# An attention layer in banded steps: query factors and the high parts of streamed weights formed on GpSimd, three key copies on ScalarE, in place of VectorE

## The chip, the cores and the metric

The program runs on one core of one Trainium2 chip. A core has five engines that each work through a queue of their own in order: TensorE (PE in the profile, its weight loads PEld), VectorE (DVE), ScalarE (ACT), GpSimd (POOL) and SyncE (SP), which only issues transfers. The metric is the time of one execution in microseconds; the median of the runs is compared.

## What is computed

A trunk of two layers on 1024 tokens of width 1024 in float32. Layer 0 mixes tokens by a gated short convolution, layer 1 by attention in a sliding window of 128 with 16 query heads, 4 key heads and head width 64; a SwiGLU channel mixer follows each. Cut to the attention, which the change touches:

```python
qkv = h @ w_qkv
q = rmsnorm(q, q_gain)                   # over each head's 64 numbers
k = rmsnorm(k, k_gain)
scores = jnp.einsum('bnqkgd,bnskd->bnkgqs', qb, kw).astype(jnp.float32) * scale
alibi = -slopes[:, :, None, None] * dist.astype(jnp.float32)[None, None]
scores = scores + alibi[None, None]
scores = jnp.where(mask[None, :, None, None], scores, -jnp.inf)
logits = jnp.concatenate([scores, sink_col], axis=-1)
p = jax.nn.softmax(logits, axis=-1)[..., :-1]
out = jnp.einsum('bnkgqs,bnskd->bnqkgd', p.astype(vw.dtype), vw)
return out.reshape(bsz, s, N_Q_HEADS * HEAD_DIM) @ w_o
```

## The kernel before

Every float32 product is made of three matmuls of a faster format (fp32r): each operand is split into a high part (a cast, hi) and a low part (the number less its high part, lo), and hi x hi, hi x lo and lo x hi are summed. Large products are further cut by a scheme of seven products of quarter matrices, so that some weights are streamed as sums of quarters.

The attention layer is `attention_layer`. Keys and values are projected first, under a planner that gives each piece a due time. Then the instructions are issued by hand, in an order written out (`manual_schedule`), and each engine's queue is just what was issued to it. This part makes the queries of eight pairs of heads, and at the same time works the heads already made, in steps of one unit (head i, block b of 128 queries). One call of `step` goes through the letters of `ORDER = "ASPTMEDkPHLVOPK"`: for step n, A forms the distances of unit n+2 (GpSimd, L2261 and L2264: distance times a factor `away` of the head), S the scores of unit n (PE, L2249 and L2250, into the only bank P0), P one piece of the pair product (PE, L2036: 12 matmuls for each granule of streamed weights, taken from a doubled buffer WL), T turns the exponentials of unit n-2 (PE, L2305), M takes the scores and distances together and finds their maxima (VectorE, L2276), E the exponentials of unit n-1 (ScalarE, L2296), D the divisions that are due, k and K what is planned for this step, H and L the high and low part of the turned unit n-2 (ScalarE L2312, VectorE L2318), V the values' product of unit n-3 (PE, L2331 and L2332), and O its copy out (ScalarE L2349, VectorE L2350).

The divisions begin with the sink of two heads' half: `mx` less the sink (GpSimd, L2360), its exponential (ScalarE, L2361), added to the sums `den` (GpSimd, L2362). Later the inverse sums are spread (GpSimd, L1822), turned (PE, L1827) and multiplied in (VectorE, L2378).

Planned work is of four kinds. `split_granule` splits the next granule of streamed weights, hi on VectorE (L1979) and lo on GpSimd (L1980). `keep_q` makes a head's query tile: squares on ScalarE, their sums on PE (L1678), the mean `hr_m` on VectorE (L1719), its logarithm (ScalarE, L1697) and with an exponential (L1702) a first guess `hr_y` of the inverse root; VectorE squares it (L1704), improves it by a Newton step (L1724, L1725) and forms `away` (L1728). `keep_q` also splits the raw queries, in quarters, hi on ScalarE (L2202) and lo on GpSimd (L2207). `part` makes the key operands of two groups of heads g in halves e: a copy on ScalarE (L1912), a copied high part on VectorE (L1914), the low part on GpSimd (L1917), and a copy of it on ScalarE. `split_o` splits the finished output (ScalarE L2460, GpSimd L2461).

Of the kernel before, what the change touches and what calls it, by code (L numbers as in the profile page):

```python
# [15 lines left out]
P = 128  # L16
# [71 lines left out]
def trunk_kernel(ctx: ExitStack, tc: tile.TileContext, xT, small, w_in, w_out, w_q, w_v, w_o, w_gu, w_dn, out):  # L88
# [1571 lines left out]
    def attention_layer():  # L1660
# [39 lines left out]
        def head_guess(y):  # L1700

            act.activation(y, y, AF.Exp, scale=-0.5)  # L1702
            t = slot("hr_t", (P, NB, 2), bufs=2)
            dve.tensor_tensor(t, y, y, ALU.mult)  # L1704
            return t
# [13 lines left out]
                    dve.scalar_tensor_tensor(m[to, :, sub], src[of, :, e], 1.0 / HD, it["eps_q"][to, :, sub], ALU.mult, ALU.add)  # L1719
            return m  # L1720

        def query_newton(i, y, t, m):

            dve.scalar_tensor_tensor(t, t, 0.5, m, ALU.mult, ALU.mult)  # L1724
            dve.scalar_tensor_tensor(y, t, 1.5, y, ALU.subtract, ALU.mult)  # L1725
            minus[i] = y
            away[i] = slot("away", (P, NB, 2), bufs=3)
            dve.scalar_tensor_tensor(away[i], m, cst[:, C_NEGS + i : C_NEGS + i + 1], y, ALU.mult, ALU.mult)  # L1728

        minus = {}  # L1730
        away = {}
# [126 lines left out]
        def keys_and_values():  # L1858


            def load(name, src, n, t):
                def f():
                    it[name] = Weights()
                    nc.sync.dma_start(it[name].raw.rearrange("p (k c) -> p k c", k=n), src)

                at(t, f)

            def split_v(q):
                raw = it["wv", q].raw
                hi, lo = (slot(f"G{8 + 2 * i + q}", dtype=F32R) for i in (0, 1))  # L1870
                dve.tensor_copy(hi, raw)
                dve.tensor_tensor(lo, raw, plain(hi), ALU.subtract)
                it.setdefault("wv", []).append((hi, lo))

            t = begin
            at(t - 150.0, act.preload_act_table_set, "natural_log_exp_and_others")
            at(t - 20.0, constants)
            at(t + 9.0, lambda: nc.sync.dma_start(x_aside, X[NK - 1]))
            for q in (0, 1):
                load(("wv", q), w_v[:, 4 * q : 4 * q + 4, :], 4, t + (-14.0, -12.5)[q])  # L1880
                at(t + (-9.3, -6.6)[q], split_v, q)
            operand_sums(0, ("A2", "A3"), t - 4.6)
            operand_sums(1, ("A0", "A1"), t + 1.5)
            operand_sums(2, ("A4", "A5"), t + 8.0)

            def mean():
                ps = bank("P3")
                for b in range(NB):
                    c = slice(b % 4 * P, (b % 4 + 1) * P)
                    pe.matmul(ps[:, b : b + 1], state["ss", b // 4][:, c], ones, start=True, stop=True)  # L1890
                it["ps"] = ps

            def token_rows():
                m = slot("rs_m", (P, NB))
                it["r"], it["eps"] = slot("r", (P, NB)), slot("eps_r", (P, NB))
                dve.tensor_scalar(m, it["ps"][:, 0:NB], 1.0 / D, EPS, ALU.mult, ALU.add)
                dve.tensor_scalar(it["eps"], m, EPS, None, ALU.mult)
                it["eps_q"] = slot("eps_q", (P, NB, 2))
                for e in range(2):
                    for sub in range(2):  # L1900
                        of = it["eps"][sub * SUB : (sub + 1) * SUB, :]
                        dve.tensor_copy(it["eps_q"][e * SUB : (e + 1) * SUB, :, sub], of)
                rsqrt(it["r"], m, (P, NB))

            def part(g, e, i):
                if g not in kz:
                    kz[g] = pair_slot(f"A{g}"), pair_slot(f"A{g + 2}")
                hi, lo = kz[g]
                raw = key_raw[g]
                rows, rest = (slice(x * HD, (x + 1) * HD) for x in (e, 1 - e))  # L1910
                if i == 0:
                    act.copy(hi[rows, e, :], raw[rows, :])  # L1912
                elif i == 1:
                    dve.tensor_copy(hi[rest, e, :], raw[rows, :])  # L1914
                elif i == 2:
                    eng = dve if (g, e) == (0, 0) else pool
                    eng.tensor_tensor(lo[rows, e, :], raw[rows, :], plain(hi[rows, e, :]), ALU.subtract)  # L1917
                else:
                    act.copy(lo[rest, e, :], plain(lo[rows, e, :]))

            it["part"] = part

            def project_values(q):
                def f():
                    it["v", q] = project_v(q)

                line.work(51, f)

            project_values(0)
            line.work(4, mean)  # L1930
            at(line.end + 0.05, token_rows)
            project_values(1)
            operand_sums(3, ("G8", "G10", "G9", "G11"), line.end + 0.1)
            first_pairs()
# [104 lines left out]
        def first_pairs():  # L2039
# [61 lines left out]
            for j in range(n_first):  # L2101
                begins[j] = line.end
                u, k = seq[j]
                for p in range(NK // 2):
                    line.work(3, of_product, j, p)
                    if p == 1 and j == 7:
                        rows_work(0, 0)
                    if p == 1 and j == 8:
                        stats_work(1)
                    if p == 1 and j == 10:  # L2110
                        rows_work(1, 1)
                    if (j, p) in ((11, 3), (12, 0), (12, 1), (12, 2)):
                        line.work(1, first.stats, {(11, 3): 4, (12, 0): 6, (12, 1): 0, (12, 2): 2}[j, p], 2)
                    if (j, p) == (12, 2):
                        for d, f in ((0.1, first.mean), (0.5, first.guess), (0.9, first.newton)):
                            at(line.end + d, f)
                t = line.end
                finish(u, k, lambda f, t=t: at(t + 0.05, f))
                if j in (4, 6):
                    g = 0 if j == 4 else 1  # L2120
                    for h in (0, 1):
                        at(t + 0.8 + 0.65 * h, squares, g, h)
                if j == 5:
                    stats_work(0)
                if j in (7, 9):
                    rows_work(*{7: (0, 1), 9: (1, 0)}[j])
                if j == 9:
                    for i, d in enumerate((0.7, 0.06, 1.6, 3.1)):
                        at(t + d, it["part"], 0, 0, i)
                if j == 10:  # L2130
                    at(t + 0.4, keep_v, 0, 0)
                    at(t + 0.8, first.squares1)
                if j == 11:
                    at(t + 0.75, first.squares0)
                    at(t + 0.8, keep_v, 0, 1)
# [27 lines left out]
        def keep_q(i, raw_of, side=None, later=0, hold=0, steps=False):  # L2163
# [3 lines left out]
            def squares(h):  # L2167
                if "raw" not in t:
                    t["raw"] = raw_of()
                    wide = slot(f"G{5 + i % 2}") if side is None else side  # L2170
                    t["side"] = [wide[:, h * 512 : h * 512 + 512] for h in (0, 1)]
                act.activation(t["side"][h], t["raw"][:, h * 512 : h * 512 + 512], AF.Square)
# [8 lines left out]
                t["m"] = query_mean(t["st"])  # L2181
                t["y"] = head_log(t["m"])

            def guess():
                t["t"] = head_guess(t["y"])

            def newton():
                query_newton(i, t["y"], t["t"], t["m"])


            def halves(e):
# [17 lines left out]
            if steps:  # L2209
                return SimpleNamespace(  # L2210
                    squares1=lambda: squares(1),
                    squares0=lambda: squares(0),
                    stats=stats_of,
                    mean=mean,
                    guess=guess,
                    newton=newton,
                    hi0=lambda: part_hi(0, 0),
                    hi1=lambda: part_hi(0, 1),
                    hi2=lambda: part_hi(1, 0),
                    hi3=lambda: part_hi(1, 1),  # L2220
                    lo0=lambda: part_lo(0, 0),
                    lo1=lambda: part_lo(0, 1, dve),
                    lo2=lambda: part_lo(1, 0),
                    lo3=lambda: part_lo(1, 1),
                )
            for d, f in ((1, lambda: squares(0)), (1.5, lambda: squares(1)), (2.5, stats_of), (2.5, mean), (3, guess), (3, newton)):
                plan(d + later, f)
            for n, (h, e) in enumerate(((0, 0), (0, 1), (1, 0), (1, 1))):
                d = later + hold + 2 + n + 0.5 * (n > 0)
# [173 lines left out]
        def plan(d, f):  # L2403

            agenda.setdefault(pos["step"] + d, []).append(f)
# [91 lines left out]
        def work_of_pairs():  # L2497
            n = 0
            for j in range(n_first, len(seq)):
                u, k = seq[j]  # L2500
                plan(0, lambda j=j: split_granule(j + 1, dve, pool) if j > n_first else None)
                if j > n_first:
                    load_granule(j + 2)
                for p in range(NK // 2):
# [200 lines left out]
```

## Time and profile before

| | |
|---|---|
| median of 3 runs | 1939.04 us (1938.13 to 1940.21) |
| the profiled execution | 1940.18 us, its span 1938.4 us |
| TensorE's mean granted clock in it | 0.994 |
| busy: TensorE, VectorE, ScalarE, GpSimd | 1915.6, 1331.7, 893.1, 348.2 us |

The attention steps lie between about 1020 and 1210 us of the span. A row of a timeline reads: start in us, duration in us, engine, line, operation, output <- inputs, shape, and in brackets how long the engine stood idle before it and on which instruction it waited. A row of a group reads: line, engine, operation, number of instructions, then total busy us and mean ns, then the idle time in front of them and what ended it. A row of waits gives the total us, the number of times and the longest. A row of stretches gives the length, the busy time of PE, PEld, DVE, ACT and POOL with the number of instructions, then TensorE's granted clock (1.00 is full speed), the DMA engines' share and GB/s.

### The profile page before, as it was taken

Reading aid. Unit: us, or ns where it says so; the run is one execution under the profiler, and the core shown is the slowest. Engines: PE = TensorE matmul, PEld = TensorE weight load, DVE = VectorE, ACT = ScalarE, POOL = GpSimd, SP = SyncE. Lnnn points to the kernel's source line nnn. Section 1 sums busy time; section 2 is a strip of 40 time slices with the busy share of each in tenths; the row PEclk is TensorE's granted clock in tenths of the full one; section 3 lists DMA queues with packets and bytes.
Section 4 is the critical chain, followed back from the end, with each engine's and each line's share of the span. In section 5 each row is a group of like instructions: output and inputs, shape, how many; then the busy total and the mean of one; then the engine's idle time right before and its main releaser. Section 6 shows DMA issues by size and latency. Waiting matters only on the chain.

```text
span 1938.4 us, 25422 instructions
## 1 busy us (share of the span) xinstructions
PE 1915.6 (99%) x8981; PEld 1598.1 (82%) x8981; DVE 1331.7 (69%) x2305; ACT 893.1 (46%) x1751; POOL 348.2 (18%) x450
## 2 busy tenths in 40 slices
PE   9999999999999999999998999999999999999999
PEld 7888888888888888888887887888888888888887
DVE  8898877966665656656857887788665665665543
ACT  5543564633333334544556787655333333344441
POOL 0001231012111100000016777410111111100000
PEclk9999999999999999999998999999999999999999
DMA  8897695388887739986463562142674676468563
GB/s 315 258 245 164 125 247 154 111 276 231 218 244 215 173 116 328 317 235 196 146 228 132 195 207 66 59 171 69 220 216 129 207 184 175 129 232 282 195 229 100
DMA packets 155200, 375.17 MB, mean 194 GB/s; under 512 B 15425, under 2 KB 26817, under 8 KB 155073
## 3 DMA queue, kind: packets, MB, share of 16 engines
q1 hardware_dynamic: 119680, 264.20, 40.4%
q0 software_dynamic: 35248, 109.33, 23.5%
q8 instruction: 70, 1.15, 0.2%
q14 instruction: 58, 0.47, 0.1%
q10 hardware_dynamic: 144, 0.03, 0.0%
HBM read 301.41 MB, written 149.95 MB: 233 GB/s over the span
## 4 chain that ended last, share of the span: by engine, by line
PE 94%; DVE 2%; ACT 1%; issue 1%; POOL 1%; DMA 1%; SPq 0%; POOLq 0%; ACTq 0%; DVEq 0%
PE acc L1004 16%; PE acc L1005 16%; PE acc L1007 16%; PE P L1004 10%; PE P L1007 10%; PE P L1005 10%; PE acc L171 3%; PE P L2036 2%; PE acc L2036 2%; PE acc L175 1%; PE P L2305 1%; PE acc L1137 1%; PE acc L1139 1%; PE acc L1138 1%; PE P L1678 1%
## 5 line engine op out<-in xcount | busy, mean ns | idle before, releaser
L1004 PE MATMUL acc<-XS,G 128*128 128x512 f32 x926 | 360.4, 389 | 0.0
L1005 PE MATMUL acc<-XS,G 128*128 128x512 f32 x926 | 360.2, 389 | 0.0
L1007 PE MATMUL acc<-XS,G 128*128 128x512 f32 x926 | 360.2, 389 | 0.0
L1004 PE MATMUL P<-A,G 128*128 128x512 f32 x550 | 214.1, 389 | 0.0
L1007 PE MATMUL P<-A,G 128*128 128x512 f32 x550 | 214.0, 389 | 0.0
L1005 PE MATMUL P<-A,G 128*128 128x512 f32 x550 | 214.0, 389 | 0.0
L1004 PEld LDWEIGHTS acc<-XS,G 128*128 128x128 f32 x926 | 173.8, 188 | 36.1
L1005 PEld LDWEIGHTS acc<-XS,G 128*128 128x128 f32 x926 | 173.8, 188 | 36.0
L1007 PEld LDWEIGHTS acc<-XS,G 128*128 128x128 f32 x926 | 173.8, 188 | 36.0
L1004 PE MATMUL acc<-A,G 128*128 128x512 f32 x442 | 172.1, 389 | 0.0
L1007 PE MATMUL acc<-A,G 128*128 128x512 f32 x442 | 172.0, 389 | 0.0
L1005 PE MATMUL acc<-A,G 128*128 128x512 f32 x442 | 171.9, 389 | 0.0
L938 DVE TENSOR_TENSOR G<-WR,G 128x512 fp32r<-128x512 f32 (+1 forms) x216 | 144.2, 668 | 31.9 <-ACT G L937 31.7
L938 DVE TENSOR_TENSOR G<-WL,G 128x512 fp32r<-128x512 f32 x168 | 115.0, 685 | 73.1 <-ACT G L937 73.1
L937 ACT CAST G<-WR 128x512 fp32r<-128x512 f32 (+1 forms) x216 | 130.4, 605 | 60.1 <-PE acc L1007 25.2
L937 ACT CAST G<-WH 128x512 fp32r<-128x512 f32 (+1 forms) x174 | 104.6, 601 | 82.3 <-PE acc L1007 35.9
L938 DVE TENSOR_TENSOR G<-WH,G 128x512 fp32r<-128x512 f32 (+1 forms) x174 | 115.4, 663 | 21.3 <-ACT G L937 21.2
L1339 ACT ACTIVATE G<-G 128x512 f32<-128x512 f32 x88 | 55.8, 634 | 159.2 <-DVE G L1436 152.9
L901 POOL DMA_DIRECT2D s<-s x68 | 60.1, 894 | 361.0 <-DMA s<-s 182.9
L1005 PEld LDWEIGHTS P<-A,G 128*128 128x128 f32 x550 | 103.2, 188 | 21.4
L1004 PEld LDWEIGHTS P<-A,G 128*128 128x128 f32 x550 | 103.2, 188 | 21.4
L1007 PEld LDWEIGHTS P<-A,G 128*128 128x128 f32 x550 | 103.2, 188 | 21.4
(429 smaller groups left out, 3849.5 us busy)
## 6 DMA issues: line engine op xcount, KB each, us to landing
G<-h SPq DMA_DIRECT2D x70, 512.0 KB, 5.1
s<-in_w_dn SPq DMA_DIRECT2D x32, 704.0 KB, 8.2
h<-X POOLq DMA_DIRECT2D x44, 512.0 KB, 5.5
s<-s POOLq DMA_DIRECT2D x32, 704.0 KB, 7.2
WR<-s SPq DMA_DIRECT2D x79, 256.0 KB, 4.1
WR<-in_w_gu SPq DMA_DIRECT2D x36, 512.0 KB, 4.8
WH<-in_w_gu SPq DMA_DIRECT2D x36, 512.0 KB, 4.7
XS<-q_ops SPq DMA_DIRECT2D x36, 512.0 KB, 5.2
```

The costliest lines, as they stand in the source:

```text
L171: pe.matmul(ps.half(h), wh, xs[:, j, c], start=first and j == 0, stop=False)
L175: pe.matmul(ps.half(h), wl, xs[:, 0, c], start=False, stop=last)
L901: nc.gpsimd.dma_start(dst[to], dst[of], accum_op=ALU.add)
L937: lambda: act.copy(out_hi, raw),
L938: lambda: lo_eng.tensor_tensor(out_lo, raw, plain(out_hi), ALU.subtract),
L1004: pe.matmul(ps, w[:, 0, c], x[:, 0, :], start=start and e == 0, stop=False, skip_group_check=True)
L1005: pe.matmul(ps, w[:, 0, c], x[:, 1, :], start=False, stop=False, skip_group_check=True)
L1007: pe.matmul(ps, w[:, 1, c], x[:, 0, :], start=False, stop=last, skip_group_check=True)
L1137: pe.matmul(ps, hi[:, kc], xs[:, 0, c], start=k == 0, stop=False, skip_group_check=True)
L1138: pe.matmul(ps, hi[:, kc], xs[:, 1, c], start=False, stop=False, skip_group_check=True)
L1339: state["silu"] = act.activation(x, x, AF.Silu)
L2036: pe.matmul(ps, g[:, w, c], x[:, b, :], start=begin and i == 0, stop=end and i == 2, skip_group_check=True)
```

## The change

Three things move between engines; what is computed stays the same. First, the factors of a query tile (`query_factors`, in place of `head_guess` and `query_newton` for queries) are formed by two-operand instructions and multiplications by constants, six on GpSimd where four stood on VectorE; for the first tile the six are on VectorE, at the place where its guess stood. Second, `split_granule` in the steps casts the high part on GpSimd (20 granules). Third, three of the four copied high key parts go to ScalarE.

```diff
-        def query_newton(i, y, t, m):
-
-            dve.scalar_tensor_tensor(t, t, 0.5, m, ALU.mult, ALU.mult)
-            dve.scalar_tensor_tensor(y, t, 1.5, y, ALU.subtract, ALU.mult)
+        def query_factors(i, y, m, eng):
+
+            act.activation(y, y, AF.Exp, scale=-0.5)
+            t = slot("hr_t", (P, NB, 2), bufs=2)
+            eng.tensor_tensor(t, y, y, ALU.mult)
+            eng.tensor_tensor(t, t, m, ALU.mult)
+            eng.tensor_scalar(t, t, 0.5, 1.5, ALU.mult, ALU.subtract)
+            eng.tensor_tensor(y, y, t, ALU.mult)
             minus[i] = y
             away[i] = slot("away", (P, NB, 2), bufs=3)
-            dve.scalar_tensor_tensor(away[i], m, cst[:, C_NEGS + i : C_NEGS + i + 1], y, ALU.mult, ALU.mult)
+            eng.tensor_tensor(away[i], m, y, ALU.mult)
+            eng.tensor_scalar(away[i], away[i], cst[:, C_NEGS + i : C_NEGS + i + 1], None, ALU.mult)
...
                 elif i == 1:
-                    dve.tensor_copy(hi[rest, e, :], raw[rows, :])
+                    if (g, e) == (0, 0):
+                        dve.tensor_copy(hi[rest, e, :], raw[rows, :])
+                    else:
+                        act.copy(hi[rest, e, :], raw[rows, :])
...
-                        for d, f in ((0.1, first.mean), (0.5, first.guess), (0.9, first.newton)):
+                        for d, f in ((0.1, first.mean), (0.5, first.factors)):
...
-            def guess():
-                t["t"] = head_guess(t["y"])
-
-            def newton():
-                query_newton(i, t["y"], t["t"], t["m"])
+            def factors(eng=pool):
+                query_factors(i, t["y"], t["m"], eng)
...
-                    guess=guess,
-                    newton=newton,
+                    factors=lambda: factors(dve),
...
-            for d, f in ((1, lambda: squares(0)), (1.5, lambda: squares(1)), (2.5, stats_of), (2.5, mean), (3, guess), (3, newton)):
+            for d, f in ((1, lambda: squares(0)), (1.5, lambda: squares(1)), (2.5, stats_of), (2.5, mean), (3, factors)):
...
-                plan(0, lambda j=j: split_granule(j + 1, dve, pool) if j > n_first else None)
+                plan(0, lambda j=j: split_granule(j + 1, pool, pool) if j > n_first else None)
```

The queues of PE and SP keep their content and order. ScalarE's gets three casts more and keeps its order otherwise. How VectorE's and GpSimd's change is shown at two places; the rows give line, operation, output <- inputs and shape, and line numbers after the change are 4 to 8 higher (L2264 becomes L2268, L2207 L2212, L2276 L2280, L2318 L2322, L2350 L2354, L2360 L2364, L2361 L2365, L1980 L1988).

VectorE before, where the third head's factors are formed (about 1070 us of the span; P and acc are banks, G and A buffers, ISA is the maxima's own instruction):

```order
L1719 SCALAR_TENSOR_TENSOR hr_m_8832<-P_1252_8823,eps_q_8005 64x8 x4
L2318 TENSOR_TENSOR G_1255_8841<-P_1251_8816,G_1255_8841 128x256
L2350 TENSOR_TENSOR G_1220_8577<-acc_8419,G_1220_8577 64x2x2x64
L1704 TENSOR_TENSOR hr_t_8854<-hr_y_8837 128x16
L1724 SCALAR_TENSOR_TENSOR hr_t_8854<-hr_t_8854,hr_m_8832 128x16
L1725 SCALAR_TENSOR_TENSOR hr_y_8837<-hr_t_8854,hr_y_8837 128x16
L1728 SCALAR_TENSOR_TENSOR away_8858<-hr_m_8832,cst_61,hr_y_8837 128x16
L2276 ISA G_1189_8375,mx_8472<-P_1258_8862,G_1189_8375,cst_61,hr_y_8567 128x192
```

VectorE after, at the same place:

```order
L1719 SCALAR_TENSOR_TENSOR hr_m_8836<-P_1252_8827,eps_q_8005 64x8 x4
L2322 TENSOR_TENSOR G_1255_8845<-P_1251_8820,G_1255_8845 128x256
L2354 TENSOR_TENSOR G_1220_8579<-acc_8421,G_1220_8579 64x2x2x64
L2280 ISA G_1190_8381,mx_8474<-P_1258_8868,G_1190_8381,cst_61,hr_y_8569 128x192
L2280 ISA mx_8474 128x1
```

The four factor instructions are gone, and the maxima stand right behind the copy out.

GpSimd before, at the same place (s, G and X here are the score buffers that distances go to; mx and den belong to the sink):

```order
L2264 TENSOR_TENSOR G_1189_8375<-cst_61,away_8589 128x2x192
L2207 TENSOR_TENSOR G_1249_8802<-G_1177_8277,G_1249_8802 64x8x64
L2264 TENSOR_TENSOR X_1190_8376<-cst_61,away_8589 128x2x192
L2360 TENSOR_TENSOR mx_8472<-mx_8472,cst_61 128x16
L2362 TENSOR_TENSOR den_8495<-den_8495,mx_8472 128x16
```

(Between the last distance and mx another pair of L2207 and L2264 with the same names stands, left out here as it only repeats.) GpSimd after, with the pair left out likewise:

```order
L1726 TENSOR_TENSOR hr_t_8858<-hr_y_8841 128x16
L1727 TENSOR_TENSOR hr_t_8858<-hr_t_8858,hr_m_8836 128x16
L1728 TENSOR_SCALAR hr_t_8858<-hr_t_8858 128x16
L1729 TENSOR_TENSOR hr_y_8841<-hr_y_8841,hr_t_8858 128x16
L1732 TENSOR_TENSOR away_8863<-hr_m_8836,hr_y_8841 128x16
L1733 TENSOR_SCALAR away_8863<-away_8863,cst_61 128x16
L2212 TENSOR_TENSOR G_1249_8806<-G_1177_8277,G_1249_8806 64x8x64
L2268 TENSOR_TENSOR X_1191_8382<-cst_61,away_8592 128x2x192
L2364 TENSOR_TENSOR mx_8474<-mx_8474,cst_61 128x16
L2366 TENSOR_TENSOR den_8497<-den_8497,mx_8474 128x16
```

The six factor instructions stand between the distance to G (the row in front of them, as before) and the low query part, so everything down to the sink's `mx` comes behind them. The cast of a granule's high part is a further row, right in front of its L1988.

ScalarE before, where the sink is taken at this place:

```order
L1702 ACTIVATE hr_y_8837<-hr_y_8837 128x16
L2296 ACTIVATE s_1188_8374,den_8495<-s_1188_8374,mx_8472 128x192 x2
L2202 CAST G_1249_8802<-G_1177_8277 64x8x64
L2312 CAST G_1260_8881<-P_1259_8870 128x512
L2349 COPY G_1219_8576<-P_1261_8884 64x2x2x64
L2296 ACTIVATE G_1189_8375,den_8495<-G_1189_8375,mx_8472 128x192 x2
L2361 ACTIVATE mx_8472<-mx_8472 128x16
L2202 CAST G_1264_8915<-G_1177_8277 64x8x64
L2312 CAST G_1265_8919<-P_1263_8903 128x512
```

This order is the same after the change, under the new line numbers: the sink's exponential stands ahead of the next high query part and the next turned unit.

## The prediction

> **What bounds the kernel now.** I read the page's busy times first, then busy time and granted clock by stretches of 100 us, then what TensorE (PE) waited for, and last the timeline of each engine around the longest waits.
>
> ```profile
> PE 1915.6 (99%) x8981; PEld 1598.1 (82%) x8981; DVE 1331.7 (69%) x2305; ACT 893.1 (46%) x1751; POOL 348.2 (18%) x450
> ...
> 1000.00:1100.00 100.00, 90.19 (x503) 76.43 (x501) 71.28 (x185) 67.15 (x178) 60.78 (x64) 0.91 0.48 159
> 1100.00:1200.00 100.00, 93.61 (x612) 82.06 (x610) 83.00 (x243) 77.47 (x234) 77.36 (x89) 0.97 0.44 145
> 1200.00:1300.00 100.00, 99.31 (x548) 84.39 (x546) 82.22 (x183) 59.69 (x156) 36.64 (x56) 1.00 0.31 109
> ...
> PE P L2249 <- DVE mx L2276: 12.2, 10, 3.2
> PE acc L2036 <- POOL WL L1980: 2.5, 2, 2.3
> PE P L2249 <- POOL G L2207: 1.3, 1, 1.3
> ```
>
> TensorE is busy for 99% of the span, so only its idle and its slow time can be won. Both lie in 1000 to 1200 us, the attention stage: 9.81 + 6.39 = 16.2 us idle, and a granted clock of 0.91 and 0.97 (the number before the last two of a row), so about 11 us more lost to the clock (0.09 of 90 us and 0.03 of 94). Nearly all the idle has one form, the scores (L2249) waiting for VectorE's maxima (L2276). The largest but one of these, on all engines:
>
> ```profile
> 1071.25 0.97 DVE L1704 TENSOR_TENSOR hr_t<-hr_y 128x16 f32<-128x16 f32 x1
> 1072.25 0.18 DVE L1724 SCALAR_TENSOR_TENSOR hr_t<-hr_t,hr_m 128x16 f32<-128x16 f32 x1
> 1072.46 0.68 DVE L1725 SCALAR_TENSOR_TENSOR hr_y<-hr_t,hr_y 128x16 f32<-128x16 f32 x1
> 1073.18 1.30 DVE L1728 SCALAR_TENSOR_TENSOR away<-hr_m,cst,hr_y 128x16 f32<-128x16 f32 x1
> 1074.52 0.48 DVE L2276 CUSTOM_DVE_ANT_0 G<-P,G,cst 128x192 f32<-128x192 f32 x1
> ...
> 1069.98 0.83 POOL L2264 TENSOR_TENSOR G<-cst,away 128x384 f32<-128x384 f32 x1
> 1070.89 1.29 POOL L2207 TENSOR_TENSOR G<-G,G 64x512 fp32r<-64x512 f32 x1
> 1072.26 0.85 POOL L2264 TENSOR_TENSOR X<-cst,away 128x384 f32<-128x384 f32 x1
> 1073.19 1.26 POOL L2207 TENSOR_TENSOR G<-G,G 64x512 fp32r<-64x512 f32 x1
> ...
> 1070.58 0.22 ACT L1702 ACTIVATE hr_y<-hr_y 128x16 f32<-128x16 f32 x1
> ...
> 1072.95 0.36 ACT L2349 COPY G<-P 64x256 f32<-64x256 f32 x1
> ...
> 1075.55 0.33 PE L2249 MATMUL P<-A,G 128*128 128x192 f32 x1 [2.95 <-DVE mx L2276]
> ```
>
> Four VectorE instructions on 128x16 numbers, one of which needs 0.18 us when nothing disturbs it, hold VectorE for 3.2 us. L1704 ends at 1072.22, GpSimd's L2207 at 1072.18; L1725 ends at 1073.14, L2264 at 1073.11; L1728 at 1074.48, the next L2207 at 1074.45. They end when the GpSimd (POOL) instruction beside them ends. Behind them stand the maxima, behind these the scores' bank: PE waits 2.95 us. I call this place D. The clock falls behind such waits:
>
> ```profile
> 1036.00:1046.00 10.00, 9.48 (x37) 8.69 (x38) 5.35 (x13) 3.21 (x10) 9.01 (x8) 0.51 0.17 53
> 1050.00:1053.00 3.00, 3.00 (x12) 2.54 (x11) 2.33 (x7) 1.99 (x3) 0.00 (x0) 0.50 0.00 0
> 1077.00:1080.00 3.00, 3.00 (x14) 2.71 (x13) 2.31 (x8) 1.86 (x6) 1.28 (x1) 0.51 0.06 24
> 1127.00:1133.00 6.00, 6.00 (x42) 5.29 (x42) 5.51 (x16) 5.16 (x16) 3.81 (x5) 1.00 0.37 138
> 1176.00:1183.00 7.00, 5.92 (x22) 5.24 (x23) 4.62 (x14) 3.65 (x11) 6.44 (x10) 0.51 0.00 0
> ...
> 1036.52 0.80 PE L2036 MATMUL acc<-XS,WL 128*128 128x512 f32 x1 [2.26 <-POOL WL L1980]
> ...
> 1049.15 0.36 PE L2249 MATMUL P<-A,G 128*128 128x192 f32 x1 [1.85 <-DVE mx L2276]
> ...
> 1126.60 0.36 PE L2249 MATMUL P<-A,G 128*128 128x192 f32 x1 [2.59 <-DVE mx L2276]
> ...
> 1177.08 0.53 PE L2249 MATMUL P<-A,G 128*128 128x192 f32 x1 [3.16 <-DVE mx L2276]
> ```
>
> Call these places A (1036), B (1049), E (1126) and F (1177). Half clock follows A, B, D and F, not E: 10, 3, 3 and 7 us of it cost 5, 1.5, 1.5 and 3.5 us. [...]
>
> **The change part by part.** *Factors.* Seven tiles' four VectorE instructions go (those of the first tile stay). At B, D, E and F the maxima come at once: 1.85 + 2.95 + 2.59 + 3.16 = 10.55 us of idle goes if nothing else is late, with 1.5 + 1.5 + 3.5 = 6.5 us of half clock behind it.
>
> ```profile
> L1980 POOL TENSOR_TENSOR WL<-WR,WL 128x512 fp32r<-128x512 f32 x21 | 27.4, 1306 | 36.9 <-DVE WL L1979 14.8 <-PE P L2250 8.9 <-ACT WL L1979 6.5
> L1979 DVE CAST WL<-WR 128x512 fp32r<-128x512 f32 x20 | 10.7, 535 | 0.4
> L1822 POOL COPY s<-den 128x512 f32<-128x512 f32 x15 | 9.2, 612 | 11.6 <-PE P L1827 9.4 <-DVE den L2367 2.2
> L2360 POOL TENSOR_TENSOR mx<-mx,cst 128x16 f32<-128x16 f32 x8 | 1.7, 216 | 2.8 <-ACT G L2296 1.6 <-ACT XS L2296 1.2
> L1912 ACT CAST A<-G 64x1024 fp32r<-64x1024 f32 x3 | 3.1, 1040 | 0.1
> ```
>
> GpSimd gets six small instructions for each of seven tiles. The nearest row is L2360, 0.216 us; with the 0.03 us between neighbours, six are 6 x 0.25 = 1.5 us. The upper end would be six of L1822's 0.61, 3.7 us, but those have 32 times the elements, so I take 1.5.
>
> What is late next is GpSimd itself, which works in order. At D the first of the six waits for ScalarE's exponential (L1702, ends 1070.80); then the six to 1072.35, L2207 (1.29 and 0.07 between) to 1073.7, a distance (L2264, 0.83) to 1074.6, the second L2207 to 1075.9, a distance to 1076.8, and only then the sink's subtraction (mx, L2360). ScalarE's exponential of the sink (L2361) needs it and stands ahead of the next high query part (L2202) and the next tile's turned scores (L2312), which VectorE and PE wait for. Without the stall ScalarE, through with L2349 at 1073.3, needs four exponentials of 1.0 us together and comes to L2361 at 1074.3: it waits 2.7 us. The next such place, one tile later, call H:
>
> ```profile
> 1095.53 0.22 ACT L1702 ACTIVATE hr_y<-hr_y 128x16 f32<-128x16 f32 x1
> ...
> 1096.53 0.20 ACT L2361 ACTIVATE mx<-mx 128x16 f32<-128x16 f32 x1
> ...
> 1098.63 0.42 DVE L2318 TENSOR_TENSOR G<-P,G 128x256 fp32r<-128x256 f32 x1
> ...
> 1099.85 0.28 PE L2331 MATMUL P<-G,A 128*128 128x256 f32 x1
> ```
>
> After the change: exponential to 1095.75, six to 1097.25, L2207 to 1098.6, a distance to 1099.45, the subtraction to 1099.7. L2361 moves from 1096.53 to 1099.75, 3.2 us. The turned scores' low part (L2318) ended at 1099.05 and the values (L2331) began at 1099.85, so 0.8 us is cover by this path. The bounds are 1.5 us (L2361, L2202 and L2312 run one behind the other to 1100.95, the low part to 1101.4, and the values follow at once) and 3.2 us (no cover, since VectorE's next maxima stand behind that low part). I take 3.2 - 0.9 = 2.3 us, near the cover seen. It comes three times (tiles 3, 5, 7). No stall stands there now, so nothing pays for it. At D the same cover of 0.6 to 0.9 us leaves about 2.1 us; E has the same order and gets 2.1 too.
>
> ```profile
> 1179.93 0.21 ACT L2361 ACTIVATE mx<-mx 128x16 f32<-128x16 f32 x1 [2.29 <-POOL mx L2360]
> ```
>
> At F ScalarE waits for the sink already. Its subtraction moves 1.5 us later, and ScalarE, no longer held by the stall, comes some 3 us sooner: 1.5 + 2.9 = 4.4 us of wait less 0.8, 3.6 us for PE, and half clock behind it again (3.5 us).
>
> *Casts.* Twenty casts go from VectorE to GpSimd. No cast on GpSimd is in the trace: bounds are VectorE's own 0.43 (a quiet one; mean 0.535) and L1980's 1.306, a two-input instruction of that size; L1822 has one input and the same size, so I take 0.61. L1980 now waits for VectorE's cast, 14.8 us in 21 cases, 0.7 us each, so the cast takes the place of a wait. At A,
>
> ```profile
> 1032.41 2.38 POOL L1917 TENSOR_TENSOR A<-G,A 64x1024 fp32r<-64x1024 f32 x1
> 1034.86 1.60 POOL L1980 TENSOR_TENSOR WL<-WR,WL 128x512 fp32r<-128x512 f32 x1
> ```
>
> the granule's low part stood behind a key part. VectorE's instructions beside it go, L1980 falls from 1.60 towards 1.31, and the granule before it is through earlier: between 0 and 2.26 us; I take half, 1.2, and let the half clock stay.
>
> *Key copies.* Three copies of 1.04 us (L1912's row) go to ScalarE, 67% busy there: hidden by its idle time. At B GpSimd stays the limit, since six factor instructions follow its 2.4 us key part; of 3.35 us I take back 0.35.
>
> The sum, gain positive: A 1.2; B 1.85 + 1.5 - 0.35 = 3.0; D 2.95 + 1.5 - 2.1 = 2.35; E 2.59 - 2.1 = 0.5; F 3.16 + 3.5 - 3.6 - 3.5 = -0.45; H 3 x -2.3 = -6.9. Together -0.3. The profiled run took 1940.18 us, 1.1 above the median of 1939.04, so 1940.5 becomes **1939** among unprofiled runs.
>
> **The rivals.** *Faster: the sink's wait is covered.* If ScalarE's lead and PE's other products take up half of the new waits (2.1 + 2.1 + 3.6 + 3.5 + 6.9 = 18.2, half 9.1), the time is 1930; all of it, 1921. For it: VectorE and ScalarE are idle for 17 to 33% of the stage, and L2361 waits 2.29 us at F with the loss there put down to something else. Against: the 0.8 us of cover at H.
>
> *Slower: the sink holds ScalarE.* Without cover D, E, F cost 0.6 + 0.7 + 0.8 us more and H 3 x 0.9, 4.8 in all; and idle of 3.2 us at H is longer than B's 1.85, so half clock follows three times, 3 x 1.5. That is 1939 + 4.8 + 4.5 = 1948; with half of it 1944. It decides from the point where ScalarE's delay exceeds about 1.6 us. For it: the queue orders are fixed. Against: E, where 2.59 us was not followed by half clock.
>
> *GpSimd's casts are dear.* At 1.306 instead of 0.61 the four granules around A and B take 2.8 us more: GpSimd is busy for 9.01 of 10 us there. 1942 to 1943.
>
> *The clock falls on its own.* If the fall at B and D is not from the wait, 3 us of the gain stay away: 1942. E, idle without a fall, speaks for it; four of five waits followed by one speak against. [...]
>
> **How the numbers follow.** A measurement of this kernel tells about 0.2%, 3.9 us, from no change: under 1935.2 is faster, over 1942.9 slower. The forecast has a chance of 0.36, the covered wait 0.32 (faster), the held ScalarE 0.20 (slower), dear casts 0.07 (slower), the clock on its own 0.05 (half of it slower). So faster 0.32, same 0.39, slower 0.29. The forecast's own range is 1934 to 1944; the range for 8 in 10 reaches into the covered wait, to 1927, and to the end of the held ScalarE, 1948.
>
> **What would show it.** Right: no VectorE instruction of 128x16 numbers over 0.3 us in the stage but the first tile's; PE's wait for the maxima under 5 us in total; ScalarE's wait for the sink, 6.4 us before, at 15 to 25 us; GpSimd's cast at 0.6 us. Wrong: a wait for the sink under 10 us, or PE not late by it (faster); half clock at H, or over 0.9 us for a cast or 0.4 us for a factor instruction on GpSimd (slower).

## The result: slower by 0.6%

The changed kernel took 1950.05 us (median of 4 runs, 1948.18 to 1952.93) against 1938.59 us before: a ratio of 1.006, with a 95% interval of 1.0043 to 1.0078. The profiled execution took 1952.93 us, 12.7 more than that of before. 1939 was forecast and 1927 to 1948 given as the range, so the time lies outside it, and near the 1948 of the rival in which the sink holds ScalarE. One run of the kernel before, in the series of the first experiments, was in a slow state at 8380.6 us and is in no comparison below. Both kernels make the large products in fp32r alike, and no run here makes them in float32, so what that format gains is not shown, and the comparison does not need it.

The profile after, first by busy time in the same stretches, then what TensorE waited for:

```profile
PE 1924.6 (99%) x8981; PEld 1604.0 (82%) x8981; DVE 1304.5 (67%) x2256; ACT 894.9 (46%) x1754; POOL 369.1 (19%) x512
...
1000.00:1100.00 100.00, 89.91 (x507) 75.55 (x505) 55.15 (x161) 68.14 (x176) 69.26 (x91) 0.93 0.49 165
1100.00:1200.00 100.00, 93.27 (x560) 80.47 (x560) 66.86 (x203) 72.73 (x220) 82.43 (x113) 0.90 0.43 139
1200.00:1300.00 100.00, 96.49 (x541) 82.39 (x541) 75.54 (x177) 60.24 (x166) 41.79 (x63) 0.98 0.28 95
```
```profile
PE P L2335 <- ACT G L2316: 5.9, 4, 1.9
PE P L2335 <- DVE A L2354: 5.2, 2, 2.8
PE acc L2044 <- POOL WL L1987: 2.6, 1, 2.6
PE P L2253 <- DVE mx L2280: 2.5, 6, 1.1
```

VectorE lost 16 us of work in each of the first two stretches, as meant, and TensorE gained nothing by it over the stage as a whole. The wait for the maxima fell from 12.2 to 2.5 us. In its place the values' product (L2335) waits for the turned scores' high part (ScalarE, L2316) and for the copy out (L2354), which stands behind the low part on VectorE. TensorE stands idle for 20.3 us in these 300 us (before 16.9), and its clock is lower from 1100 on: 0.90 and 0.98, before 0.97 and 1.00.

Who holds ScalarE is seen in the waits of ScalarE, and in GpSimd's groups of the factors:

```profile
ACT mx L2365 <- POOL mx L2364: 23.4, 8, 4.8
```
```profile
L1726 POOL TENSOR_TENSOR hr_t<-hr_y 128x16 f32<-128x16 f32 x7 | 1.5, 215 | 17.8 <-ACT hr_y L1724 13.0 <-DVE G L2322 4.7
L1733 POOL TENSOR_SCALAR away<-away,cst 128x16 f32<-128x16 f32 x7 | 2.3, 330 | 0.7
L1987 POOL CAST WL<-WR 128x512 fp32r<-128x512 f32 x20 | 12.2, 612 | 3.5 <-PE acc L2044 3.0
```

ScalarE waited 23.4 us for the sink (6.4 before). In front of the first of the six instructions GpSimd stood idle for 17.8 us, 2.5 us for each of seven tiles. The row names VectorE for 4.7 us of it, but in all seven tiles that first instruction starts within 0.1 us of the end of ScalarE's guess, so it is the guess that it waits for. The six themselves take less, 1.5 us a tile (0.215 to 0.330 us each), 1.9 with the gaps between them. A GpSimd cast took 0.612 us, as taken.

At H (the fourth head) the timeline of GpSimd, ScalarE and TensorE reads:

```profile
1093.72 0.21 POOL L1726 TENSOR_TENSOR hr_t<-hr_y 128x16 f32<-128x16 f32 x1 [2.98 <-ACT hr_y L1724]
...
1095.72 1.28 POOL L2212 TENSOR_TENSOR G<-WH,G 64x512 fp32r<-64x512 f32 x1
1097.08 0.82 POOL L2268 TENSOR_TENSOR s<-cst,away 128x384 f32<-128x384 f32 x1
1097.86 0.22 POOL L2364 TENSOR_TENSOR mx<-mx,cst 128x16 f32<-128x16 f32 x1
...
1098.12 0.21 ACT L2365 ACTIVATE mx<-mx 128x16 f32<-128x16 f32 x1 [3.60 <-POOL mx L2364]
1098.35 0.61 ACT L2207 CAST G<-WH 64x512 fp32r<-64x512 f32 x1
1098.99 0.37 ACT L2316 CAST G<-P 128x256 fp32r<-128x256 f32 x1
...
1099.42 0.38 PE L2335 MATMUL P<-G,A 128*128 128x256 f32 x1 [1.93 <-ACT G L2316]
```

GpSimd waits for the guess, forms the factors, the low query part and a distance, and gets to the sink 3.6 us after ScalarE; the high part is late by that, and the values with it. After this wait, and after the same wait two heads later, the clock is down:

```profile
1100.00:1104.00 4.00, 4.00 (x14) 3.04 (x15) 2.70 (x10) 3.95 (x13) 3.77 (x5) 0.50 0.18 58
1155.00:1160.00 5.00, 5.00 (x18) 3.84 (x17) 3.47 (x12) 4.32 (x13) 4.73 (x6) 0.50 0.19 65
```

What a place costs is read by following one and the same matmul through both traces. The scores that begin before H and after it, before the change:

```profile
1095.00 0.25 PE L2249 MATMUL P<-A,G 128*128 128x192 f32 x1
...
1121.57 0.25 PE L2249 MATMUL P<-A,G 128*128 128x192 f32 x1
```

and after the change:

```profile
1092.90 0.25 PE L2253 MATMUL P<-A,G 128*128 128x192 f32 x1
...
1124.32 0.25 PE L2253 MATMUL P<-A,G 128*128 128x192 f32 x1
```

26.57 us became 31.42: H costs 4.85 us. How much of this is idle time and how much is slower work is read from the stretches between the same scores, for the three tiles at which H comes, before the change:

```profile
1095.00:1121.57 26.57, 26.19 (x179) 22.95 (x177) 23.87 (x73) 20.68 (x67) 17.45 (x22) 1.00 0.56 181
1144.56:1167.05 22.49, 22.13 (x147) 19.12 (x146) 20.75 (x61) 19.55 (x61) 19.38 (x23) 1.00 0.51 162
1201.48:1241.39 39.91, 39.22 (x251) 34.24 (x250) 32.03 (x92) 28.06 (x92) 23.73 (x33) 1.00 0.09 28
```

and after it:

```profile
1092.90:1124.32 31.42, 29.41 (x179) 25.52 (x178) 22.03 (x66) 20.87 (x67) 22.73 (x32) 0.89 0.48 149
1147.48:1174.84 27.36, 25.36 (x147) 21.70 (x146) 18.72 (x54) 19.77 (x61) 24.52 (x33) 0.88 0.41 132
1209.24:1253.80 44.56, 41.05 (x252) 35.46 (x251) 31.95 (x92) 27.95 (x92) 26.64 (x36) 0.96 0.08 25
```

The length of a stretch less PE's busy time is TensorE's idle time. It grew from 0.38, 0.36 and 0.69 us to 2.01, 2.00 and 3.51, by 6.1 us in all. The three stretches grew by 14.4 us; the other 8.3 go to the same matmuls, slower at a granted clock of 0.89, 0.88 and 0.96 in place of 1.00.

All places in the same way (start of the same scores in both traces, us of the span; gain positive):

```
place    from..to before     predicted   measured
A        ..1043.1               1.2        -0.45
B        1043.1..1070.2         3.0         2.3
D        1070.2..1095.0         2.35        0.25
H 1st    1095.0..1121.6        -2.3        -4.85
E        1121.6..1144.6         0.5        -0.2
H 2nd    1144.6..1167.1        -2.3        -4.85
F        1167.1..1201.5        -0.45        0.05
H 3rd    1201.5..1241.4        -2.3        -4.65
sum                            -0.3       -12.4
```

### The profile page after: what moved, and what is told of

Read it like the earlier page. It is cut to its first block, busy times and chain, and to the rows that moved or that the text cites. A ratio compares the mean times of both kernels' runs of the same rounds, so it can differ in the third digit from the quotient of the medians.

```text
span 1950.8 us, 25467 instructions
## 1 busy us (share of the span) xinstructions
PE 1924.6 (99%) x8981; PEld 1604.0 (82%) x8981; DVE 1304.5 (67%) x2256; ACT 894.9 (46%) x1754; POOL 369.1 (19%) x512
## 3 DMA queue, kind: packets, MB, share of 16 engines
q8 instruction: 70, 1.15, 0.2%
## 4 chain that ended last, share of the span: by engine, by line
PE 93%; POOL 3%; DVE 1%; issue 1%; ACT 1%; POOLq 0%; DVEq 0%; ACTq 0%
PE acc L1004 16%; PE acc L1005 16%; PE acc L1007 16%; PE P L1004 9%; PE P L1005 9%; PE P L1007 9%; PE acc L171 2%; PE P L2044 2%; PE acc L2044 2%; POOL G L2212 1%; PE acc L175 1%; PE P L2309 1%; PE acc L1137 1%; PE acc L1138 1%; PE acc L1139 1%
## 5 line engine op out<-in xcount | busy, mean ns | idle before, releaser
L938 DVE TENSOR_TENSOR G<-WH,G 128x512 fp32r<-128x512 f32 (+1 forms) x174 | 115.7, 665 | 20.3 <-ACT G L937 20.2
```

Source lines behind the costliest of these rows:

```text
L938: lambda: lo_eng.tensor_tensor(out_lo, raw, plain(out_hi), ALU.subtract),
```

## The experiments

**Casts alone.** Of the change only the twenty casts are made.

```diff
-                plan(0, lambda j=j: split_granule(j + 1, dve, pool) if j > n_first else None)
+                plan(0, lambda j=j: split_granule(j + 1, pool, pool) if j > n_first else None)
```

> Only the casts of the streamed weights' high parts move to GpSimd; factors and key copies stay on VectorE. Theory (the loss of the change is the sink's wait behind the factors): the casts alone cost nothing, ScalarE's wait for the sink stays near 6.4 us, 1936 to 1940 us. Rival (a busier GpSimd is the loss): ScalarE's wait for the sink doubles and the time is 1943 us or more.

1930.99 us, ratio 0.9969 (0.9958 to 0.9980): 7.1 us faster than the kernel before (1938.11 us in this series), better than either theory said. ScalarE's wait for the sink was 6.6 us. Two things make up most of the gain of the profiled execution, which is 9.8 us. One shows at E (2.4 us). Before, VectorE's rows there, and GpSimd's a little earlier, read

```profile
1122.41 0.95 DVE L1704 TENSOR_TENSOR hr_t<-hr_y 128x16 f32<-128x16 f32 x1
1123.39 0.17 DVE L1724 SCALAR_TENSOR_TENSOR hr_t<-hr_t,hr_m 128x16 f32<-128x16 f32 x1
1123.60 0.69 DVE L1725 SCALAR_TENSOR_TENSOR hr_y<-hr_t,hr_y 128x16 f32<-128x16 f32 x1
1124.33 1.30 DVE L1728 SCALAR_TENSOR_TENSOR away<-hr_m,cst,hr_y 128x16 f32<-128x16 f32 x1
...
1119.89 1.29 POOL L1980 TENSOR_TENSOR WL<-WR,WL 128x512 fp32r<-128x512 f32 x1 [3.77 <-DVE WL L1979]
```

and with the casts on GpSimd

```profile
1117.98 0.16 DVE L1704 TENSOR_TENSOR hr_t<-hr_y 128x16 f32<-128x16 f32 x1
1118.17 0.18 DVE L1724 SCALAR_TENSOR_TENSOR hr_t<-hr_t,hr_m 128x16 f32<-128x16 f32 x1
1118.38 0.17 DVE L1725 SCALAR_TENSOR_TENSOR hr_y<-hr_t,hr_y 128x16 f32<-128x16 f32 x1
1118.59 0.23 DVE L1728 SCALAR_TENSOR_TENSOR away<-hr_m,cst,hr_y 128x16 f32<-128x16 f32 x1
...
1116.40 0.82 POOL L2264 TENSOR_TENSOR X<-cst,away 128x384 f32<-128x384 f32 x1
1119.18 1.28 POOL L2207 TENSOR_TENSOR G<-G,G 64x512 fp32r<-64x512 f32 x1 [1.95 <-PE P L2331]
```

GpSimd no longer waits for VectorE's cast, is through with its earlier work sooner, and does nothing beside these four: they take 0.7 us in place of 3.1, and the wait of 2.59 us is gone. TensorE's wait for the maxima fell to 8.0 us in 4 cases (12.2 in 10).

At D and F the four instructions still take 2.4 and 2.6 us (3.1 and 3.0 before), and the gain there, 2.6 and 2.7 us, is mostly the other thing, a clock that did not fall. With the casts on GpSimd:

```profile
1000.00:1100.00 100.00, 90.69 (x529) 77.37 (x528) 69.43 (x186) 70.89 (x189) 70.57 (x79) 0.95 0.51 169
1100.00:1200.00 100.00, 96.08 (x642) 84.13 (x641) 81.06 (x248) 79.48 (x245) 85.30 (x105) 1.00 0.43 138
...
1050.00:1053.00 3.00, 2.79 (x18) 2.53 (x19) 2.68 (x9) 2.95 (x8) 1.69 (x3) 1.00 0.00 0
...
1050.21 0.36 PE L2249 MATMUL P<-A,G 128*128 128x192 f32 x1 [2.97 <-DVE mx L2276]
```

TensorE's idle time in 1000 to 1300 us fell by only 3.7 us (16.9 to 13.2), while its clock rose from 0.91 to 0.95 and from 0.97 to 1.00. At B TensorE even waits longer than before, 2.97 in place of 1.85 us, yet no half clock follows (1.00 in the row above), nor does it after 1.88 us at D, where the scores' matmuls (L2250) take 0.27 or 0.28 us in the 6 us behind the wait (up to 0.41 before), nor after 2.40 at F, within the 1.00 of 1100 to 1200 us; so by difference, 9.8 less 3.7, some 6 us are clock, an estimate. This is no chance of one execution: TensorE's mean granted clock lay at 0.995 to 0.998 in the eight runs and at 0.993 to 0.996 in the 23 of the kernel before. What keeps the clock up is not shown.

**Factors alone.** The change without casts and key copies: `split_granule(j + 1, dve, pool)` again, and all four key copies as before.

> Only the factors of query tiles 1 to 7 move to GpSimd; casts and key copies stay on VectorE. Theory: the whole loss comes back, 1948 to 1952 us, with over 20 us of ScalarE waiting for the sink and a loss of 4 to 5 us at each of the three odd tiles. Rival (casts and factors only together overfill GpSimd): under 1944 us.

1956.22 us, ratio 1.0098 (1.0084 to 1.0112): slower than the whole change, and 4 us above the range that was expected, though ScalarE's wait for the sink (24.0 us) and the loss at each of the three odd tiles (4.5 to 4.7 us) came as expected. The factors cost 18.1 us, and the other two parts take back 6.

**Casts and key copies.** The change without the factors.

```diff
-                plan(0, lambda j=j: split_granule(j + 1, dve, pool) if j > n_first else None)
+                plan(0, lambda j=j: split_granule(j + 1, pool, pool) if j > n_first else None)
...
-                    dve.tensor_copy(hi[rest, e, :], raw[rows, :])
+                    if (g, e) == (0, 0):
+                        dve.tensor_copy(hi[rest, e, :], raw[rows, :])
+                    else:
+                        act.copy(hi[rest, e, :], raw[rows, :])
```

> Casts on GpSimd and the three key copies on ScalarE; all factors on VectorE as before. Theory: the copies are hidden on ScalarE and relieve VectorE once, at the second tile: within 1.5 us of the casts alone (1931 us), rather below. Rival: the copies make ScalarE late there, 1932.5 us or more.

1930.01 us, ratio 0.9959 (0.9945 to 0.9972). The key copies' share, 1.0 us, is within the intervals.

**The factors behind the sink.** The same instructions on the same engines as in the change; only GpSimd's six are issued later.

```diff
-            act.activation(y, y, AF.Exp, scale=-0.5)
...
+            def guess():
+                act.activation(t["y"], t["y"], AF.Exp, scale=-0.5)
...
-            for d, f in ((1, lambda: squares(0)), (1.5, lambda: squares(1)), (2.5, stats_of), (2.5, mean), (3, factors)):
+            for d, f in ((1, lambda: squares(0)), (1.5, lambda: squares(1)), (2.5, stats_of), (2.5, mean), (3, guess), (4.5, factors)):
```

> The whole change, but GpSimd's six factor instructions are issued 1.5 steps later, behind the sink's subtraction; ScalarE's exponential stays where it is, so the same work stands on every engine. Theory: ScalarE's wait for the sink falls under 8 us, the 4.8 us lost at each of three odd tiles and about 2 us at each of three even ones go, 1926 to 1934 us. Rival (GpSimd's load, not its order): still over 1945 us. Second rival: the next tile's distances become late instead, between.

1934.56 us, ratio 0.9983 (0.9974 to 0.9992): 15.5 us below the change, with the same work on every engine. So the amount of work that GpSimd has is not what costs the time; the place at which it stands is. ScalarE's wait for the sink fell to 10.6 us, not under 8, and the time stayed 0.6 us above the expected range:

```profile
ACT mx L2367 <- POOL mx L2366: 10.6, 8, 3.8
```

What is left stands at F and at the last tile (3.7 us slower there than before). At F other work of GpSimd is ahead of the sink, two splits of the output (L2467) above all. In GpSimd's, ScalarE's and TensorE's timeline:

```profile
1167.64 1.29 POOL L2467 TENSOR_TENSOR XS<-G,XS 128x512 fp32r<-128x512 f32 x1
1169.01 1.28 POOL L2214 TENSOR_TENSOR G<-G,G 64x512 fp32r<-64x512 f32 x1
...
1171.33 0.22 POOL L2366 TENSOR_TENSOR mx<-mx,cst 128x16 f32<-128x16 f32 x1
...
1171.58 0.21 ACT L2367 ACTIVATE mx<-mx 128x16 f32<-128x16 f32 x1 [3.46 <-POOL mx L2366]
...
1174.02 0.51 PE L2337 MATMUL P<-G,A 128*128 128x256 f32 x1 [2.99 <-DVE A L2356]
```

**The wait or the work.** As the last one, and six small multiplications of constants where the change had its factors. They wait for nothing, and nothing reads them.

```diff
+            def idle_work():
+                x = slot("hr_x", (P, NK))
+                c = cst[:, C_SINK : C_SINK + NK]
+                for _ in range(6):
+                    pool.tensor_tensor(x, c, c, ALU.mult)
...
-            for d, f in ((1, lambda: squares(0)), (1.5, lambda: squares(1)), (2.5, stats_of), (2.5, mean), (3, guess), (4.5, factors)):
+            for d, f in ((1, lambda: squares(0)), (1.5, lambda: squares(1)), (2.5, stats_of), (2.5, mean), (3, guess), (3, idle_work), (4.5, factors)):
```

> As with the factors behind the sink (1934.6 us), and where the change had its six factor instructions GpSimd does six small multiplications of constants (128x8, on a tile that nothing reads), which wait for nothing. Theory (the loss is the wait for ScalarE's guess, 2.5 us a tile, together with the six instructions, 1.7 us a tile, and only what exceeds the slack counts): the work alone costs a third or less of the 15.5 us, 1935 to 1940 us. Rival (the instructions' time alone is the loss): 1945 us or more.

1940.84 us, ratio 1.0012 (1.0003 to 1.0021): 6.3 of the 15.5 us, 40%, a little over the third that was expected. Six of these multiplications take 1.6 us, near the 1.9 of the factors. ScalarE waits 15.0 us for the sink, between 10.6 and 23.4. So the six instructions' own time is the smaller part. The larger, 9.2 us, is left for GpSimd's wait for the guess, which came with them; this is a difference of two runs, not a run with the wait alone.

**The sink on VectorE.** Tried on the whole change, on the factors behind the sink, and on the casts alone.

```diff
-                pool.tensor_tensor(t, t, tiles.unsqueeze(1).to_broadcast([P, 8, 2]), ALU.subtract)
+                dve.tensor_tensor(t, t, tiles.unsqueeze(1).to_broadcast([P, 8, 2]), ALU.subtract)
```

> The whole change with its order, but the sink's subtraction (128x16) is done by VectorE instead of GpSimd, so that ScalarE waits no longer for GpSimd's queue. Theory: as with the factors behind the sink, 1926 to 1936 us, ScalarE's wait for the sink under 5 us. Rival (ScalarE and PE would be late by the low query parts and distances behind the factors anyway): over 1943 us.

> The whole change with GpSimd's factors 1.5 steps later and the sink's subtraction on VectorE. In the run with the factors behind the sink, 4.7 us at the seventh tile and 3.7 us at the last were still lost while ScalarE waited 3.5 us and more for the sink behind two splits of the output on GpSimd. Theory: these go too, 1924 to 1929 us. Rival (VectorE now waits for, or is held by, something else): 1932 us or more.

> Only the casts on GpSimd, and the sink's subtraction on VectorE; factors and key copies on VectorE as before. Theory: ScalarE's wait for the sink, 6.6 us with the casts alone, is off TensorE's path but at the seventh tile: 1929 to 1931 us, within 2 us of the casts alone. Rival: VectorE is the late engine at the factors, and a further instruction there makes it slower, 1932 us or more.

On the whole change 1937.38 us (ratio 0.9995, 0.9986 to 1.0004): 12.7 us are won back without moving a factor, the whole loss, so it is the sink that carries it. But this is 1.4 us above what was expected, and ScalarE still waits 12.9 us for it. With the factors behind the sink as well, 1934.3 us (0.9980, 0.9971 to 0.9988), no better than 1934.56: the expectation of 1924 to 1929 fell, and ScalarE waits 11.1 us for the sink there. With the casts alone, 1937.69 us (0.9996, 0.9987 to 1.0005), 6.7 us slower than without it. The groups of ScalarE's exponential and of the subtraction in that last run show what became of the wait:

```profile
L2361 ACT ACTIVATE mx<-mx 128x16 f32<-128x16 f32 x8 | 1.7, 215 | 14.8 <-DVE mx L2360 14.8
L2360 DVE TENSOR_TENSOR mx<-mx,cst 128x16 f32<-128x16 f32 x8 | 1.5, 188 | 0.0
```

The subtraction takes 0.19 us and VectorE is never idle in front of it, yet ScalarE waits 14.8 us: on VectorE it stands behind what is issued there ahead of it, the factors and the maxima of the newest unit. The wait had only changed its queue. TensorE's wait for the maxima, 8.0 us with the casts alone, is 12.7 here.

**A version built from these.** Two further steps on casts and key copies: the granule at A split by VectorE, and the second tile's factors, whose VectorE form lies beside GpSimd's 2.4 us key part, on GpSimd 1.5 steps later.

```diff
-                plan(0, lambda j=j: split_granule(j + 1, pool, pool) if j > n_first else None)
+                plan(0, lambda j=j: split_granule(j + 1, *((dve, dve) if j == n_first + 2 else (pool, pool))) if j > n_first else None)
```

> Casts on GpSimd and key copies on ScalarE, factors on VectorE, and the one granule for which TensorE waits behind GpSimd's key part (about 1035 us; 2.3 to 2.9 us of idle in every kernel so far, about 10 us of half clock behind it) is split by VectorE, high and low part. Theory: the wait falls under 1 us and the half clock there goes: 1930 less 2 to 7, 1923 to 1928 us. Rival (VectorE's two-input split ends only with the GpSimd instruction beside it, or the half clock stays): 1929 us or more.

1928.6 us, ratio 0.9949 (0.9936 to 0.9963), just above the 1923 to 1928 that were expected. The wait at A is gone, but TensorE then waits up to 2.9 us for the maxima at B, and the granted clock of 1036 to 1046 us, of which it stands idle for 2.62, is 0.66; against 0.9959 for casts and key copies no gain can be told.

```diff
-            for d, f in ((1, lambda: squares(0)), (1.5, lambda: squares(1)), (2.5, stats_of), (2.5, mean), (3, guess), (3, newton)):
+            for d, f in ((1, lambda: squares(0)), (1.5, lambda: squares(1)), (2.5, stats_of), (2.5, mean), (3, guess), ((4.5, factors) if i == 1 else (3, newton))):
```

> The same, and the second tile's factors (whose VectorE form waits beside a 2.4 us key part of GpSimd) are formed by GpSimd behind the sink's place, 1.5 steps later. Theory: the wait for the maxima at the second tile goes: 1 to 4 us below the run with one granule on VectorE. Rival: GpSimd's key part and granule stand behind it and are late instead: the same or slower.

1925.75 us, ratio 0.9930 (0.9918 to 0.9943): all its runs lie below all those of the step before, and it beats both kernels. The wait for the maxima at the second tile is gone; one of 2.9 us for a low query part (L2227) comes in its place. TensorE's waits in it:

```profile
PE P L2268 <- POOL G L2227: 2.9, 1, 2.9
PE P L2268 <- DVE mx L2295: 2.7, 6, 0.9
```

## Why the prediction was wrong

*What bounds the kernel*: right. VectorE's four factor instructions held the maxima; without them TensorE's wait for these fell from 12.2 to 2.5 us.

*The new wait*: right in place and kind. The sink behind the factors on GpSimd, and ScalarE behind the sink, was worked out to 3.2 us at H and measured as 3.6; 15 to 25 us of waiting were forecast and 23.4 came. The experiments with the factors behind the sink and with the sink on VectorE show it as the cause of the loss.

*Its price at H*: here the sum failed. "I take 3.2 - 0.9 = 2.3 us" set the idle time, 6.9 us for the three tiles, and the half clock behind it was put at nothing. The idle time was about right: 6.1 us more were measured. The half clock that the sum left out cost 8.3 us, so H cost 14.4 in place of 6.9. These 7.5 us are the greater part of the 12.1 by which the sum was off. The slower rival had this term. Its condition, idle longer than B's 1.85 us, was met: one wait of 1.93 us at the first two tiles, 2.37 and 1.15 us at the third. The forecast's own 2.3 us met it too, and four of the five waits in its rows had half clock behind them. The one row against, E with its 2.59 us, was given too much weight.

*D*: 2.35 forecast, 0.25 measured. The stall went (3.7 us gained), but 3.4 came back, where 2.1 was taken: the clock fell behind the new waits too. At E the same waits came without that:

```profile
1078.00:1083.00 5.00, 4.71 (x21) 3.85 (x20) 3.59 (x13) 3.94 (x11) 4.76 (x8) 0.66 0.18 56
1134.00:1139.00 5.00, 4.71 (x30) 3.71 (x29) 4.16 (x14) 4.83 (x14) 4.76 (x8) 1.00 0.29 77
```

Around the start of the first stretch (D) TensorE waited 1.02, 0.34 and 0.29 us, around that of the second (E) 1.03, 0.34 and 0.29.

*E and F*: within 0.7 us. At F this is in part luck: about 4.3 us were gained and lost again, where the sum had 6.7 and 7.1.

*A*: 1.2 forecast, -0.45 measured. GpSimd's cast stands behind the key part as L1980 did, and TensorE waits 2.6 us for it.

*B*: 3.0 forecast, 2.3 measured. The second tile's factors put GpSimd's next key part off, and ScalarE's high query part waited 1.7 us for it.

*Casts*: the duration was right, 0.612 us, and the effect too small: 1.2 us was given, 7.1 measured when nothing else is changed. The step overlooked that GpSimd, once ahead, no longer runs beside VectorE's factors at E, and that half clock behind B, D and F could go. The first of these had nothing to act on in the change itself, where the factors had left VectorE; there the casts and the key copies together were worth 6 us. *Key copies*: nothing, as forecast, within the intervals.

The parts had the right signs in the sum, 1.2 us gained by the casts and 1.5 lost net at the places of the factors, but both were far too small: 7.1 us gained and 18.1 lost when each is made alone.

## What to carry to other kernels

Moving an instruction to an idle engine moved its wait too: GpSimd stood still for 2.5 us a tile while the first factor instruction waited for the guess, and what was queued behind it was late, whoever wanted it; at H ScalarE waited 3.6 us for the sink. So before moving, name what stands behind the new place, and put the moved work just behind the most urgent of it; here 1.5 steps, with no instruction more or fewer, were worth 15.5 us. Where the trace shows the clock halve after short waits, give a new wait two prices, with half clock behind it and without, and let the range hold both: at H 6.1 us of idle time brought 8.3 us of slower work (0.50 behind the wait), at E the same waits as at D brought none (1.00, at D 0.66).

## What was not expected

VectorE's four instructions on 128x16 numbers took 0.16 to 0.23 us at E with the casts alone, where GpSimd stood idle, and up to 1.30 us before the change beside one of its usual instructions (at D beside an L2207 of 1.26 us; 2.24 us at B, beside a key part of 2.65 us), so that relieving VectorE of a cast made other VectorE instructions four times as short at E (3.1 to 0.7 us).

In these traces the length of a wait alone does not decide whether the clock falls. It did after 1.93 us at H (to 0.50) and around the group at D (1.02, 0.34 and 0.29 us; 0.66), and it did not after 2.59 us at E before the change or after 2.97 us at B with the casts alone (1.00 both times). What decides was not tried and stays open.
